# The diagonal-block forward substitution of a gated-delta network, for two batches at once on 128 lanes

## The chip, the cores and the metric

The kernel runs on one core of one Trainium2 chip. The metric is device time in microseconds (us) of one execution: median 3812.47 over three runs (3810.61 to 3817.99). PE is TensorE, DVE is VectorE, ACT is ScalarE, POOL is GpSimd, SP is SyncE, which issues the transfers (DMAs).

## The reference, cut to what matters

Two layers of a transformer-like block over 256 context tokens and 1024 latent tokens (1280 in all), width 1024, float32. A layer projects the normed tokens once; the columns go to four groups of heads (HGRN2, retention, gated delta, S5), each scanned in both directions; then an output projection and an MLP. The change lies in the gated-delta group: 4 heads of 64 columns, chunks of 64 tokens, so 20 chunk steps in a direction. Per chunk:

```
g = cumsum(log_a)
lmat = where(tri, exp(min(g_i - g_j, 0)), 0)
a_mat = where(strict, (k*beta) @ k^T * lmat, 0)
u, w = solve(a_mat + I, [v*beta, k*beta*exp(g)])      # unit lower triangular, 64x64
qk = where(tri, q @ k^T * lmat, 0);  q_dec = q*exp(g)
v_new = u - w @ s
o = q_dec @ s + qk @ v_new
s = s*exp(g_last) + k_dec^T @ v_new                   # the state, chunk after chunk
```

## The kernel before, in words

Each layer runs in stages. The stage that matters here has two streams of work. One is the gated-delta group: `gdn_conv` (a convolution on DVE, transposes `gd_pt` on PE, products of keys `gd_kk`, kept in DRAM as `kk` and `kv`), `gdn_stats` (the cumulated decays: products `gd_g` on PE, copies `gd_gp` and `gd_gc` on DVE, decay rows kept in DRAM as `gr`), and `gdn_main`, the 20 steps. The other, called the filler, is the rest of the input projections (`proj_steps`, products `pj_ps` at L1608 with evictions `pj_z`): hundreds of matrix products of 512, 272 or 256 columns that depend on nothing in the group. They are laid between the group's products, and all of them must be done before the stage's tiles are freed and the next stage begins.

`gdn_main` handles the 20 steps in five batches of four (`BS`). For a batch, `front` (L794) loads the key products M, the query products A and the queries QD, and the decay rows E; DVE subtracts (L824), ACT takes Abs and Exp, DVE and POOL multiply M (L826, L827), A (L829, L830) and QD (L822) by decays. The inverse of each unit triangular 64x64 block is built from 32x32 blocks. The two diagonal ones are inverted by forward substitution: 4 steps x 2 directions x 4 heads x 2 diagonal blocks = 64 small matrices, each laid flat on one lane (partition) of the tile `gd_TL`. To get there M is written to the DRAM scratch `lanes` (four DMAs, L838) and read back (L840). The substitution is 60 DVE instructions (L846 multiplies into `gd_tmp`, L847 adds, j = 1..30), each needing the one before it. Then a transposing copy `gd_TLt` (L850), two writes to DRAM and twelve loads into the tiles `gd_TT` and `gd_XX`. `back` (L866) computes the off-diagonal block from these on PE (32 products `gd_py` L877, 32 `gd_pz`). `step` (L898) is the chain: products `gd_p` with the state (L919), DVE `gd_pre` (L924), products with the inverse (L933), DVE `gd_Vn` (L936), products into the new state (L944), DVE `gd_S` (L950, L952), and the outputs `gd_po`.

The order on every engine is fixed when the program is built: a scheduler simulates the program and lays each engine's instructions in one sequence, in which they then run. Steps have priority over fronts, and the filler has the lowest. Tiles of one name share buffers in rotation: `gd_M` has 3, `gd_E` 2, `gd_ge` 1. In layer 0 every batch has A and QD; in layer 1 the first batch has none, since the context's output is not needed there.

Of the kernel before, what the change touches and what calls it, by code (L numbers as in the profile page):

```python
# [16 lines left out]
def host_consts():  # L17
# [4 lines left out]
    c['sel8'] = (np.arange(8)[:, None, None] == np.arange(4)[None, :, None] * 2 + (i // 64)[None, None, :]).astype(f)  # L22
# [125 lines left out]
def hgrn(k, l, need_ctx):  # L148
# [11 lines left out]
    def products(key, query, other=0):  # L160
        """key^T query per 64 tokens: partition (token half, key), free (head pair, 128 tokens, head parity, query)"""
# [289 lines left out]
def hg_params(k):  # L451
    """forget gate constants a = (1-lb)/2, b = (1+lb)/2 per layer"""
# [33 lines left out]
def ret_params(k):  # L486
    """log decays, per head on every partition [l, d, h] and per partition pair [l, d, k]"""
# [16 lines left out]
def ret_tables(k):  # L504
    """decay tables of both layers: within a chunk [head pair, head, query], of queries [d, head pair, query], of keys [d, head]"""
# [200 lines left out]
def gdn_stats(k, l):  # L706
    """decays and step sizes per step, head pair and direction"""
# [73 lines left out]
def gdn_main(k, l, need_ctx, fp):  # L781
    """chunked delta rule: both directions and all heads step together"""
# [11 lines left out]
    def front(b0):  # L794
        full = need_ctx or b0 >= 4
        w = {}
        lo = [min(chunk_of(b0, d), chunk_of(b0 + BS - 1, d)) for d in range(2)]
        quad = lambda nm, bufs, f=early: f(nm, [128, 2, BS, 2, 64], bufs)
        by_chunk = lambda a, d: a[:, b0:b0 + BS, :, d] if d == 0 else rev(a[:, b0:b0 + BS, :, d], 1)
        half = [128, BS, 2, 64]  # L800
        M = w['M'] = quad('gd_M', k.gM)
        tiles = [(M, k.kk[l][:, :, 0])]
        if full:
            A, QD = w['A'], w['QD'] = quad('gd_A', k.gA), quad('gd_QD', k.gQ)
            tiles += [(A, k.kk[l][:, :, 1]), (QD, k.kv[l][:, :, 3])]
        for t, src in tiles:
            for d in range(2):
                nc.sync.dma_start(t[:, d].rearrange('p n h c -> p n (h c)'),
                                  src[lo[d]:lo[d] + BS].rearrange('n p h c -> p n (h c)'))
        Es = []  # L810
        for d in range(2):
            Es.append(early('gd_E', half, 2))
            for y in range(2):
                nc.sync.dma_start(Es[d][64 * y:64 * y + 64].rearrange('p n h c -> p (n h c)'),
                                  bc(k.gr[l][y:y + 1, d, lo[d]:lo[d] + BS].rearrange('a n h c -> a (n h c)'), [64, BS * 128]))
        for d in range(2):
            E = Es[d]
            ef = E.rearrange('p n h c -> p (n h c)')
            if full:
# [3 lines left out]
            nc.vector.tensor_tensor(E, E, bc(by_chunk(Gp, d)[:, :, :, None], half), op=SUB)  # L823
# [3 lines left out]
            nc.gpsimd.tensor_tensor(M[:, d], M[:, d], bc(by_chunk(B2, d)[:, :, :, None], half), op=MULT)  # L827
            if full:
                nc.vector.tensor_tensor(A[:, d], A[:, d], bc(k.c['gmask'][:, d, None, None], half), op=MULT)  # L829
                nc.gpsimd.tensor_tensor(A[:, d], A[:, d], E, op=MULT)  # L830
        lanes = k.lanes[k.li % len(k.lanes)]
        k.li += 1
        blk = lambda y, b: (slice(64 * y + 32 * b, 64 * y + 32 * b + 32), slice(32 * b, 32 * b + 32), (2 * y + b) * 16)
        flat = lambda a: a.rearrange('p d n h c -> p (d n h) c')
        for y in range(2):
            for b in range(2):
                p, c, L0 = blk(y, b)
                nc.sync.dma_start(lanes[0, L0:L0 + 16].rearrange('x r c -> r x c'), flat(M[p])[:, :, c])  # L838
        TL, tmp = ln('gd_TL'), early('gd_tmp', [128, 256], 1)
        nc.sync.dma_start(TL[:nl], lanes[0])  # L840
        diag = lambda t: t[:nl].rearrange('p r c -> p (r c)')[:, ::33]
        eng = nc.gpsimd if b0 // BS in k.psolve else nc.vector
        for j in range(1, 31):
            sh = [nl, 31 - j, j]
            u = tmp[:nl, :(31 - j) * j].rearrange('p (r c) -> p r c', c=j)
            eng.tensor_tensor(u, bc(TL[:nl, j + 1:, j:j + 1], sh), bc(TL[:nl, j:j + 1, :j], sh), op=MULT)  # L846
            eng.tensor_tensor(TL[:nl, j + 1:, :j], TL[:nl, j + 1:, :j], u, op=ADD)  # L847
        nc.gpsimd.memset(diag(TL), 1.0)
        TLt = ln('gd_TLt')
        nc.vector.tensor_copy(TLt[:nl], TL[:nl].rearrange('p r c -> p c r'))  # L850
        nc.sync.dma_start(lanes[1], TLt[:nl])
        nc.sync.dma_start(lanes[2], TL[:nl])
# [11 lines left out]
        return w  # L864
# [152 lines left out]
def s5_params(k):  # L1017
# [67 lines left out]
    def dbl(c, s):  # L1085
        """angle doubling"""
# [69 lines left out]
def s5_views(t):  # L1156
    """views of the parts of a quarter's tables"""
# [5 lines left out]
def s5_tables(k, l):  # L1163
    """per quarter (4 groups) of a layer: input, output and block matrices and powers of the state's decay"""
# [106 lines left out]
def s5(k, l, need_ctx):  # L1271
# [12 lines left out]
    def blocks_of(tl):  # L1284
        """tokens in blocks of 8: U [128 (token of the block, channel), group, block]"""
# [172 lines left out]
def split_st(k, st, shape):  # L1458
    """float32 -> (hi, lo) float32r tiles whose sum is exact"""
# [17 lines left out]
def mm3(k, out, terms):  # L1477
    """accumulates hi*hi + hi*lo + lo*hi over (whi, wlo, xhi, xlo), one yield per product"""
# [18 lines left out]
def modulation(k, l, r, mp, wtag, tag='mo'):  # L1497
    """a third of the shift, scale and gate vectors, channel major: k.mod[l] [128, 2 (latent, context), 48]; one yield per weight tile"""
# [31 lines left out]
def square(k, acc, x, kt, b0, bn):  # L1530
    """adds the squares of channel tile kt of the tokens [b0, b0+bn) to acc"""
# [11 lines left out]
def rnorm(k, acc, b0, bn):  # L1543
    """PSUM tile with 1/rms of the tokens [b0, b0+bn) on every partition"""
# [15 lines left out]
def norm_mod(k, X, acc, l, part, b0, bn, H):  # L1560
    """H[kt] = split of modulated norm of a block of X; part 0: first norm, 3: second"""
# [27 lines left out]
def proj_steps(k, l, H, rows, need_ctx):  # L1589
    """projections of rows, one yield per matrix product; the first two block by block"""  # L1590
# [72 lines left out]
def within(k, gen, tp, tag):  # L1663
    """runs a generator with its own pool and PSUM tag"""
# [9 lines left out]
def weave(a, b, n, c=(), m=0):  # L1674
    """a step of a, then n of b and m of c"""
# [16 lines left out]
def load_a(k, l, kts, pool, nt, blocks, pair):  # L1692
    """splits of mixer outputs"""
# [15 lines left out]
def w_out(k, l, A, blocks, start, done, few=False):  # L1709
    """start(m, block) gives the tile that the product with the rows of A is added to, done(m, block, tile) takes it"""  # L1710
# [37 lines left out]
def mlp(k, l, H, X, blocks, final):  # L1748
    """X += gated MLP; final(m, b0, bn) after the last change of a part of X, final(None, b0, bn) after a block's"""
# [64 lines left out]
def program(k):  # L1814
    from contextlib import ExitStack
    nc, tc = k.nc, k.tc
    with ExitStack() as es:
# [16 lines left out]
        k.lanes = [k.dp.tile([3, 64, 32, 32], F32, name=f'lanes{i}') for i in range(10)]  # L1834
# [42 lines left out]
        for n in ('hmask', 'heads', 'gtri', 'gmask', 'sel8', 'dmask', 'lmask'):  # L1877
# [107 lines left out]
def tune(k):  # L1985
# [7 lines left out]
    k.psolve = ()  # L1993
# [56 lines left out]
```

## Time and profile before

| | us |
|---|---|
| median of the runs | 3812.47 |
| profiled execution, span | 3814.3 |
| PE busy | 3424.2 (90%) |
| DVE busy | 2178.1 (57%) |
| POOL busy | 1148.5 |
| ACT busy | 1108.1 |
| PE's granted clock, mean | 0.940 |

The profiled execution's span of 3814.3 us is 1.8 above the median and within the range of the runs. PE is the busiest engine over the whole span, but the share of one engine is a mean over stages; the two gated-delta stages lie at about 277 to 726 us (layer 0) and 2279 to 2683 us (layer 1), and have to be read by themselves.

### The profile page before, as it was taken

What the parts mean: (1) busy time and instruction counts of PE and PEld (TensorE: products, weight loads), DVE (VectorE), ACT (ScalarE), POOL (GpSimd) and SP (SyncE); (2) the same over time, 40 slices, a digit from 0 to 9 for tenths busy, and PEclk for the clock granted to TensorE, in tenths of its full rate; (3) what the DMA queues carried; (4) which work ended last, traced back from release to release, by engine and by line L of the source; (5) the groups of instructions that cost most, each with busy time, mean ns of one, the idle gap of its engine ahead of it and who ended that gap; (6) DMA issues with size and microseconds to landing.
All of it is one profiled execution on the core that took longest, in us unless ns stands there. A gap on an engine that the chain in (4) does not pass through costs nothing. (4 is left out here: it accounts for less than half of the span.)

```text
span 3814.3 us, 60239 instructions
## 1 busy us (share of the span) xinstructions
PE 3424.2 (90%) x23367; PEld 2725.9 (71%) x23367; DVE 2178.1 (57%) x4171; ACT 1108.1 (29%) x1988; POOL 1148.5 (30%) x1202
## 2 busy tenths in 40 slices
PE   6887899788889999999998886999787799999997
PEld 3776778555667888888886785777356578888886
DVE  8968651586665344344336979741786654334445
ACT  5332212355333211221123333111463232221222
POOL 3734322254223111111112745221552231111111
PEclk7988999989999999999999988999899899999998
DMA  6565444756641111111112556444846311111111
GB/s 211 184 164 142 134 123 137 240 152 194 197 149 37 39 37 37 39 39 39 39 37 85 162 160 171 134 114 136 253 126 224 126 41 49 50 48 47 50 45 64
DMA packets 421279, 424.76 MB, mean 111 GB/s; under 512 B 185592, under 2 KB 299128, under 8 KB 419968
## 3 DMA queue, kind: packets, MB, share of 16 engines
q1 hardware_dynamic: 420992, 420.91, 36.1%
q8 instruction: 184, 3.01, 0.3%
q14 instruction: 103, 0.84, 0.1%
HBM read 308.56 MB, written 112.22 MB: 110 GB/s over the span
## 5 line engine op out<-in xcount | busy, mean ns | idle before, releaser
L1482 PE MATMUL dn_ps<-hid,w_hi 128*128 128x512 f32 (+1 forms) x2560 | 728.4, 373 | 7.9 <-DVE x L1780 7.6
L1780 DVE SCALAR_TENSOR_TENSOR x<-dn_ps,mod,x 128x512 f32<-128x512 f32 (+1 forms) x640 | 433.1, 695 | 324.3 <-PE dn_ps L1482 323.7
L1467 POOL TENSOR_TENSOR w_lo<-w_st,w_hi 128x512 fp32r<-128x512 f32 (+1 forms) x212 | 288.6, 1364 | 992.4 <-ACT w_hi L1464 978.3
L1482 PEld LDWEIGHTS dn_ps<-hid,w_hi 128*128 128x128 f32 x2560 | 463.4, 189 | 98.4 <-DVE x L1780 9.2
L1464 ACT ACTIVATE w_hi<-w_st 128x512 fp32r<-128x512 f32 (+2 forms) x408 | 249.6, 621 | 811.8 <-PE dn_ps L1482 276.3
L1482 PE MATMUL up_ps<-hlo,w_hi 128*128 128x512 f32 (+1 forms) x1280 | 475.8, 372 | 3.4 <-DVE hlo L1578 1.9
L1482 PE MATMUL up_ps<-hhi,w_hi 128*128 128x512 f32 (+1 forms) x1280 | 476.7, 373 | 2.0 <-ACT hhi L1577 2.0
L1482 PE MATMUL up_ps<-hhi,w_lo 128*128 128x512 f32 (+1 forms) x1280 | 476.2, 372 | 0.0
L1482 PE MATMUL dn_ps<-hid,w_lo 128*128 128x512 f32 (+1 forms) x1280 | 469.0, 373 | 0.0
L1608 PE MATMUL pj_ps<-hhi,w_hi 128*128 128x512 f32 (+1 forms) x960 | 369.7, 386 | 26.4 <-ACT pj_z L1586 9.5
L1608 PE MATMUL pj_ps<-hlo,w_hi 128*128 128x512 f32 (+1 forms) x960 | 367.9, 383 | 1.8 <-DVE hlo L1578 1.8
L1608 PE MATMUL pj_ps<-hhi,w_lo 128*128 128x512 f32 (+1 forms) x960 | 366.0, 382 | 1.0 <-POOL w_lo L1467 1.0
L1467 DVE TENSOR_TENSOR w_lo<-w_st,w_hi 128x512 fp32r<-128x512 f32 (+1 forms) x196 | 148.6, 763 | 314.8 <-ACT w_hi L1464 300.5
L1765 POOL TENSOR_TENSOR up_q<-up_r 128x256 f32<-128x256 f32 (+1 forms) x160 | 156.1, 976 | 566.5 <-ACT up_r L1764 479.4
L1482 PEld LDWEIGHTS up_ps<-hlo,w_hi 128*128 128x128 f32 x1280 | 242.5, 189 | 49.2 <-DVE hlo L1578 3.5
L1482 PEld LDWEIGHTS up_ps<-hhi,w_hi 128*128 128x128 f32 x1280 | 242.5, 190 | 46.5 <-ACT hhi L1577 2.8
L1482 PEld LDWEIGHTS up_ps<-hhi,w_lo 128*128 128x128 f32 x1280 | 242.2, 189 | 44.1
L1482 PEld LDWEIGHTS dn_ps<-hid,w_lo 128*128 128x128 f32 x1280 | 240.8, 189 | 45.9
L1767 DVE TENSOR_TENSOR hid<-up_q,hid 128x256 fp32r<-128x256 f32 (+1 forms) x160 | 114.1, 721 | 278.1 <-ACT hid L1766 276.0
L1608 PEld LDWEIGHTS pj_ps<-hhi,w_hi 128*128 128x128 f32 x960 | 191.2, 199 | 63.6 <-ACT pj_z L1586 10.9
L1608 PEld LDWEIGHTS pj_ps<-hlo,w_hi 128*128 128x128 f32 x960 | 191.6, 200 | 34.5 <-DVE hlo L1578 2.4
L1608 PEld LDWEIGHTS pj_ps<-hhi,w_lo 128*128 128x128 f32 x960 | 190.6, 199 | 35.6 <-issue 3.1
(401 smaller groups left out, 5964.2 us busy)
## 6 DMA issues: line engine op xcount, KB each, us to landing
w_st<-in_w SPq DMA_DIRECT2D x256, 256.0 KB, 2.6
w_mo<-in_mod_w SPq DMA_DIRECT2D x160, 256.0 KB, 3.4
w_st<-in_w_ch SPq DMA_DIRECT2D x88, 256.0 KB, 3.3
z<-pj_z SPq DMA_DIRECT2D x88, 256.0 KB, 2.9
gd_KV<-kv SPq DMA_DIRECT2D x80, 192.0 KB, 2.9
s_ta<-s5t SPq DMA_DIRECT2D x8, 1152.0 KB, 7.3
w_mo<-in_mod_w SPq DMA_DIRECT2D x16, 512.0 KB, 7.4
at<-a SPq DMA_DIRECT2D x32, 256.0 KB, 4.5
```

The costliest lines, as they stand in the source:

```text
L1464: nc.scalar.activation(fl(hi), fl(st), AF.Copy)
L1467: eng.tensor_tensor(fl(lo), fl(st), fl(hi).bitcast(F32), op=SUB)
L1482: k.nc.tensor.matmul(out, w, x, start=(i + j == 0), stop=(i == n - 1 and j == 2))
L1608: nc.tensor.matmul(ps[:, :n], x, y, start=(kt == 0 and i == 0), stop=(kt == 7 and i == 2))
L1765: nc.gpsimd.tensor_tensor(q[:, :bn], r[:, :bn], r[:, :bn], op=MULT)
L1767: nc.vector.tensor_tensor(lo[:, sl], q[:, :bn], hi[:, sl].bitcast(F32), op=SUB)
L1780: nc.vector.scalar_tensor_tensor(X(m)[:, sl], ps[:, :bn], g, X(m)[:, sl], op0=MULT, op1=ADD)
```

## The change: what it does

`front` becomes four functions. `front_m` loads M and E and multiplies M; `front_a` does A and QD, and now loads the decay rows a second time into `gd_ge` (two buffers in place of one), where before ACT computed `gd_ge` from the E tile; `solve` does the forward substitution for one batch or two; `inverses` loads `gd_TT` and `gd_XX`. `solve` runs on batches 0 and 1 together, then 2 and 3, then 4 alone, so the 60 instructions appear three times a layer in place of five, on 128 lanes in the paired cases. The scratch `lanes` is 6 tensors of 128 lanes in place of 10 of 64. A constant that nothing used (`sel8`) and a switch that chose DVE or POOL for the substitution go. The rest of the diff empties docstrings. A new layer's order: `front_m` and `front_a` of batches 0 and 1, `solve` of both, `inverses` of both, `back(0)`; then, while batch b is stepped, `inverses(b+1)`, and for even b the fronts of b+2 and b+3 and their `solve` (`front_a` of b+3 one batch later).

```diff
-    def front(b0):
-        full = need_ctx or b0 >= 4
...
-        Es = []
+    def decays(t, lo, d):
+        for y in range(2):
+            nc.sync.dma_start(t[64 * y:64 * y + 64].rearrange('p n h c -> p (n h c)'),
+                              bc(k.gr[l][y:y + 1, d, lo:lo + BS].rearrange('a n h c -> a (n h c)'), [64, BS * 128]))
+    def front_m(b):
...
+        load(M, k.kk[l][:, :, 0], lo)
+        Es = [early('gd_E', half, 2) for d in range(2)]
+        for d in range(2):
+            decays(Es[d], lo[d], d)
         for d in range(2):
...
-            if full:
-                ge = early('gd_ge', half, 1)
-                nc.scalar.activation(ge.rearrange('p n h c -> p (n h c)'), ef, AF.Exp)
-                nc.gpsimd.tensor_tensor(QD[:, d], QD[:, d], ge, op=MULT)
...
+    def front_a(b, w):
...
+            ge = early('gd_ge', half, 2)
+            decays(ge, lo[d], d)
+            gf = ge.rearrange('p n h c -> p (n h c)')
+            nc.scalar.activation(gf, gf, AF.Exp)
+            nc.gpsimd.tensor_tensor(QD[:, d], QD[:, d], ge, op=MULT)
...
+    def solve(ws):
+        n = nl * len(ws)
...
+        for i, w in enumerate(ws):
+            w['lanes'] = lanes[:, nl * i:nl * i + nl]
...
-        nc.sync.dma_start(TL[:nl], lanes[0])
+        nc.sync.dma_start(TL[:n], lanes[0, :n])
...
         for j in range(1, 31):
-            sh = [nl, 31 - j, j]
+            sh = [n, 31 - j, j]
...
+    def inverses(w):
...
-    fr = {0: front(0), 1: front(BS)}
+    for b in range(2):
+        fr[b] = front_m(b)
+        front_a(b, fr[b])
+    solve([fr[0], fr[1]])
+    for b in range(2):
+        inverses(fr[b])
     back(fr[0])
     for b in range(n):
-        if b + 2 < n:
-            fr[b + 2] = front((b + 2) * BS)
+        if b and b + 1 < n:
+            inverses(fr[b + 1])
+        if b % 2 and b + 2 < n:
+            front_a(b + 2, fr[b + 2])
+        pair = [x for x in (b + 2, b + 3) if x < n] if b % 2 == 0 else []
+        for x in pair:
+            fr[x] = front_m(x)
+            if x == b + 2:
+                front_a(x, fr[x])
+        if pair:
+            solve([fr[x] for x in pair])
```

In SP's order of layer 0, before, the four writes of batch 0's M to `lanes` are followed by a few loads and the load of `gd_TL`:

```order
L814 DMA gd_E<-gr_79 64x512 x3
L838 DMA lanes_96<-gd_M 32x16x32 x4
L814 DMA gd_E<-gr_79 64x512
L1613 DMA zr_73<-pj_z 128x256 x3
L840 DMA gd_TL<-lanes_96 64x1024
```

After, at the same place (the first `gd_TL` load of the layer; `gd_ge` are the decay rows loaded a second time):

```order
L857 DMA lanes_96<-gd_M 32x16x32 x4
L800 DMA gd_M<-kk_88 128x4x128 x2
L800 DMA gd_A<-kk_88 128x4x128 x2
L804 DMA gd_E<-gr_79 64x512 x2
L800 DMA gd_QD<-kv_92 128x4x128 x2
L804 DMA gd_ge<-gr_79 64x512 x4
L804 DMA gd_E<-gr_79 64x512
L857 DMA lanes_96<-gd_M 32x16x32 x4
L804 DMA gd_E<-gr_79 64x512
L804 DMA gd_ge<-gr_79 64x512
L859 DMA gd_TL<-lanes_96 128x1024
```

The load of `gd_TL` now stands behind the second batch's writes, and behind the loads of a third batch. From the `gr` writes to this load SP issues 54 DMAs in place of 40 in layer 0, and 48 in place of 37 in layer 1.

On DVE at the end of the first substitution of layer 0, before, the second substitution follows at once:

```order
L846 TENSOR_TENSOR gd_tmp<-gd_TL 64x30
L847 TENSOR_TENSOR gd_TL<-gd_TL,gd_tmp 64x30
L850 COPY gd_TLt<-gd_TL 64x1024
L846 TENSOR_TENSOR gd_tmp<-gd_TL 64x30
L847 TENSOR_TENSOR gd_TL<-gd_TL,gd_tmp 64x30
L846 TENSOR_TENSOR gd_tmp<-gd_TL 64x58
```

After, at the same place (`gd_Vs`, `gd_Vn` and `gd_S` are step 0 of the chain):

```order
L864 TENSOR_TENSOR gd_tmp<-gd_TL 128x30
L865 TENSOR_TENSOR gd_TL<-gd_TL,gd_tmp 128x30
L868 COPY gd_TLt<-gd_TL 128x1024
L822 TENSOR_TENSOR gd_M<-gd_M,gd_E 128x512 x2
L1619 COPY pj_z<-pj_ps 128x512
L930 TENSOR_TENSOR gd_Vs<-gd_KV,gd_st 128x256
L956 TENSOR_TENSOR gd_Vn<-gd_p_3437,gd_st 128x256
L958 TENSOR_SCALAR gd_Vn<-gd_Vn 128x256
L972 COPY gd_S<-gd_p_3437 128x256
L864 TENSOR_TENSOR gd_tmp<-gd_TL 128x30
```

The second batch's substitution is gone from here; what follows is the M of batch 3, step 0, and then the substitution of batches 2 and 3, whose instructions stand among those of step 1. On PE, the number of filler products ahead of the layer's first `gd_py` falls: in layer 0 by 15 products of 512 columns, in layer 1 by 45 of 512 and 21 of 256 columns. In layer 0, 156 filler products of 272 and 256 columns now stand between the last key products `gd_kk` and `gd_g`, where 10 stood before.

## Rows read from the trace of the kernel before

**Rows 1.** By stretch: length; busy PE, PEld, DVE, ACT, POOL; granted clock, DMA share, GB/s.
```profile
277.00:354.40 77.40, 49.54 (x277) 43.82 (x275) 65.08 (x97) 24.80 (x43) 39.47 (x35) 0.80 0.66 168
354.40:560.00 205.60, 185.98 (x2275) 149.76 (x2275) 138.20 (x350) 42.39 (x84) 61.69 (x72) 0.93 0.48 129
560.00:640.00 80.00, 80.00 (x827) 66.46 (x824) 14.28 (x45) 14.21 (x30) 15.56 (x17) 1.00 0.30 94
2362.00:2560.00 198.00, 181.61 (x1991) 143.85 (x1989) 128.85 (x338) 38.71 (x75) 58.43 (x68) 0.94 0.46 126
2560.00:2660.00 100.00, 100.00 (x988) 72.61 (x989) 17.71 (x52) 16.81 (x33) 19.23 (x21) 1.00 0.43 128
```

**Rows 2.** The substitution's instructions grouped by line: count, busy us, mean ns, idle before.
```profile
L847 DVE TENSOR_TENSOR gd_TL<-gd_TL,gd_tmp 64x30 f32<-64x30 f32 (+5 forms) x300 | 132.4, 441 | 8.7
L846 DVE TENSOR_TENSOR gd_tmp<-gd_TL 64x30 f32<-64x30 f32 (+5 forms) x300 | 129.3, 431 | 44.4 <-DMA gd_TL<-lanes 35.8
```

**Rows 3.** PE's waits, 354.4 to 560 us (layer 0): us in total, times, longest.
```profile
PE gd_py L877 <- DMA gd_TT<-lanes: 5.2, 5, 1.7
PE gd_p L933 <- DVE gd_pre L924: 3.8, 3, 1.8
PE gd_p L944 <- DVE gd_Vn L936: 3.0, 2, 1.7
PE gd_py L877 <- DMA gd_XX<-lanes: 2.8, 3, 1.9
```

**Rows 4.** PE's waits, 2362 to 2560 us (layer 1).
```profile
PE gd_p L919 <- DVE gd_S L950: 7.5, 3, 4.3
PE gd_py L877 <- DMA gd_TT<-lanes: 4.8, 3, 3.2
PE gd_p L933 <- DVE gd_pre L924: 1.9, 1, 1.9
```

**Rows 5.** DVE's timeline, two instructions on 64 and on 128 lanes: start, duration.
```profile
320.47 0.41 DVE L910 TENSOR_TENSOR gd_Vs<-gd_KV,gd_st 128x256 f32<-128x256 f32 x1
...
327.15 0.40 DVE L846 TENSOR_TENSOR gd_tmp<-gd_TL 64x238 f32<-64x238 f32 x1
```

**Rows 6.** Busy time of the instructions on `gd_tmp`, first and third substitution of layer 0.
```profile
305.80:348.10 42.30, 33.93 (x60) 0.89 0.54 144
387.70:417.40 29.70, 22.41 (x60) 1.00 0.48 134
```

**Rows 7.** PE's timeline: `gd_g`, a wait, and the first `gd_py` of either layer.
```profile
260.35 0.89 PE L760 MATMUL gd_g<-gd_st,c_gtri 64*64 64x40 f32 x16 [4.13 <-ACT gd_tk L696]
...
304.34 0.58 PE L1608 MATMUL pj_ps<-w_hi,hhi 128*128 128x256 f32 x1 [3.89 <-ACT pj_z L1586]
...
354.56 0.24 PE L877 MATMUL gd_py<-gd_TT,gd_M 32*32 32x32 f32 x2
...
2363.39 0.24 PE L877 MATMUL gd_py<-gd_TT,gd_M 32*32 32x32 f32 x2
```

**Rows 8.** Busy time of the filler's products (L1608): 512 columns, then 256, twice.
```profile
350.00:354.40 4.40, 4.40 (x21) 1.00 0.70 152
270.20:276.00 5.80, 5.80 (x51) 1.00 0.85 237
304.90:308.10 3.20, 3.20 (x17) 0.50 0.48 128
```

**Rows 9.** SP's timeline: the second batch's writes to `lanes`; layer 1's first `gd_TL` load.
```profile
315.06 0.43 SPq L838 DMA_DIRECT2D lanes<-gd_M  x1
...
2307.77 0.48 SPq L840 DMA_DIRECT2D gd_TL<-lanes  x1
...
2314.95 1.98 SPq L838 DMA_DIRECT2D lanes<-gd_M  x4
```

**Rows 10.** DVE's timeline: first instruction of layer 1's first substitution; end of layer 0's.
```profile
2313.94 1.02 DVE L846 TENSOR_TENSOR gd_tmp<-gd_TL 64x30 f32<-64x30 f32 x1
...
346.94 1.12 DVE L850 COPY gd_TLt<-gd_TL 64x1024 f32<-64x1024 f32 x1
```

More of the change, by code (lines that the diff above doesn't have):

```diff
@@ L792, in gdn_main, with load @@
     Sst = []
-    def front(b0):
-        full = need_ctx or b0 >= 4
[L796 to L802, printed above, removed]
-        if full:
[L804 to L809, printed above, removed]
-        Es = []
-        for d in range(2):
[L812 to L815, printed above, removed]
+    quad = lambda nm, bufs, f=early: f(nm, [128, 2, BS, 2, 64], bufs)
+    by_chunk = lambda a, b0, d: a[:, b0:b0 + BS, :, d] if d == 0 else rev(a[:, b0:b0 + BS, :, d], 1)
+    half = [128, BS, 2, 64]
+    lows = lambda b0: [min(chunk_of(b0, d), chunk_of(b0 + BS - 1, d)) for d in range(2)]
+    def load(t, src, lo):
+        for d in range(2):
+            nc.sync.dma_start(t[:, d].rearrange('p n h c -> p n (h c)'), src[lo[d]:lo[d] + BS].rearrange('n p h c -> p n (h c)'))
+    def decays(t, lo, d):
[3 more added lines that the diff above has]
+    def front_m(b):
+        b0 = b * BS
+        lo = lows(b0)
+        M = quad('gd_M', k.gM)
+        load(M, k.kk[l][:, :, 0], lo)
+        Es = [early('gd_E', half, 2) for d in range(2)]
+        for d in range(2):
+            decays(Es[d], lo[d], d)
         for d in range(2):
@@ L818, in front @@
             ef = E.rearrange('p n h c -> p (n h c)')
-            if full:
-                ge = early('gd_ge', half, 1)
-                nc.scalar.activation(ge.rearrange('p n h c -> p (n h c)'), ef, AF.Exp)
-                nc.gpsimd.tensor_tensor(QD[:, d], QD[:, d], ge, op=MULT)
-            nc.vector.tensor_tensor(E, E, bc(by_chunk(Gp, d)[:, :, :, None], half), op=SUB)
+            nc.vector.tensor_tensor(E, E, bc(by_chunk(Gp, b0, d)[:, :, :, None], half), op=SUB)
             nc.scalar.activation(ef, ef, AF.Abs)
@@ L826, in front @@
             nc.vector.tensor_tensor(M[:, d], M[:, d], E, op=MULT)
[L827 to L830, printed above, removed]
+            nc.gpsimd.tensor_tensor(M[:, d], M[:, d], bc(by_chunk(B2, b0, d)[:, :, :, None], half), op=MULT)
+        return dict(M=M, Es=Es)
@@ new lines, in front_a @@
+    def front_a(b, w):
+        b0 = b * BS
+        if not (need_ctx or b0 >= 4):
+            return
+        lo = lows(b0)
+        A, QD = w['A'], w['QD'] = quad('gd_A', k.gA), quad('gd_QD', k.gQ)
+        load(A, k.kk[l][:, :, 1], lo)
+        load(QD, k.kv[l][:, :, 3], lo)
+        for d in range(2):
+            ge = early('gd_ge', half, 2)
[3 more added lines that the diff above has]
+            nc.gpsimd.tensor_tensor(QD[:, d], QD[:, d], ge, op=MULT)
+            nc.vector.tensor_tensor(A[:, d], A[:, d], bc(k.c['gmask'][:, d, None, None], half), op=MULT)
+            nc.gpsimd.tensor_tensor(A[:, d], A[:, d], w['Es'][d], op=MULT)
@@ L831, in front @@
+    blk = lambda y, b: (slice(64 * y + 32 * b, 64 * y + 32 * b + 32), slice(32 * b, 32 * b + 32), (2 * y + b) * 16)
+    def solve(ws):
+        n = nl * len(ws)
         lanes = k.lanes[k.li % len(k.lanes)]
         k.li += 1
-        blk = lambda y, b: (slice(64 * y + 32 * b, 64 * y + 32 * b + 32), slice(32 * b, 32 * b + 32), (2 * y + b) * 16)
         flat = lambda a: a.rearrange('p d n h c -> p (d n h) c')
[L835 to L838, printed above, removed]
+        for i, w in enumerate(ws):
+            w['lanes'] = lanes[:, nl * i:nl * i + nl]
+            for y in range(2):
+                for b in range(2):
+                    p, c, L0 = blk(y, b)
+                    nc.sync.dma_start(w['lanes'][0, L0:L0 + 16].rearrange('x r c -> r x c'), flat(w['M'][p])[:, :, c])
@@ L848, in front @@
         nc.gpsimd.memset(diag(TL), 1.0)
         TLt = ln('gd_TLt')
-        nc.vector.tensor_copy(TLt[:nl], TL[:nl].rearrange('p r c -> p c r'))
-        nc.sync.dma_start(lanes[1], TLt[:nl])
-        nc.sync.dma_start(lanes[2], TL[:nl])
+        nc.vector.tensor_copy(TLt[:n], TL[:n].rearrange('p r c -> p c r'))
+        nc.sync.dma_start(lanes[1, :n], TLt[:n])
+        nc.sync.dma_start(lanes[2, :n], TL[:n])
+    def inverses(w):
+        lanes = w['lanes']
         TT = w['TT'] = quad('gd_TT', k.gT, tile_)
@@ L972, in gdn_main @@
     n = 20 // BS
-    fr = {0: front(0), 1: front(BS)}
+    fr = {}
+    for b in range(2):
+        fr[b] = front_m(b)
+        front_a(b, fr[b])
+    solve([fr[0], fr[1]])
+    for b in range(2):
+        inverses(fr[b])
     back(fr[0])
     for b in range(n):
-        if b + 2 < n:
-            fr[b + 2] = front((b + 2) * BS)
+        if b and b + 1 < n:
[9 more added lines that the diff above has]
+            solve([fr[x] for x in pair])
         for i in range(BS):
@@ L1833, in program @@
         xs = dt('xs', [8, 128, T])[0]
-        k.lanes = [k.dp.tile([3, 64, 32, 32], F32, name=f'lanes{i}') for i in range(10)]
+        k.lanes = [k.dp.tile([3, 128, 32, 32], F32, name=f'lanes{i}') for i in range(6)]
         k.toep = [k.dp.tile([2, 16, 2, 240], F32, name=f'toep{i}') for i in range(8)]
@@ L1876, in program @@
                 norm_mod(k, lambda kt: xt[kt], acc, 0, 0, *b, H)
-        for n in ('hmask', 'heads', 'gtri', 'gmask', 'sel8', 'dmask', 'lmask'):
+        for n in ('hmask', 'heads', 'gtri', 'gmask', 'dmask', 'lmask'):
             load_const(k, n)
@@ L1992, in tune @@
     k.nln, k.nvs = 3, 1
-    k.psolve = ()
     k.hiprio = 6000
```

11 lines of the change are left out of this document (4 added, 7 removed).

## The prediction

> **What bounds the kernel now.** I read the busy shares of the page first: PE 90%, DVE 57%. That alone says that DVE work saved is not time saved, but it is a mean over stages, so next come the busy times by stretch around the two gated-delta stages [rows 1]. Each stage has three parts. Before the chain (277 to 354.4 us in layer 0) DVE is the busiest, 65.08 of 77.40 us, and PE waits: 49.54 busy, clock 0.80. In the chain (354.4 to 560, and 2362 to 2560) PE is busy 185.98 of 205.6 and 181.61 of 198.0 us, at clock 0.93 and 0.94. After it (560 to 640, 2560 to 2660) PE is busy 80.00 of 80 and 100.00 of 100 us at clock 1.00: that is filler, products that have to be finished before the next stage, long after the last substitution. So the end of a stage is set by PE: it comes when PE has done a fixed amount of work, and moves only by what PE idles before it, or runs at the lower clock. Then I read what PE waits for in the chain [rows 3, 4], the cost of the substitution itself [rows 2, 5, 6], and what leads to the first product of the chain [rows 7 to 10].
>
> What can be won in the chain at most is therefore PE's idle time, 205.60 - 185.98 = 19.6 us in layer 0 and 198.00 - 181.61 = 16.4 in layer 1, and the time at the lower clock, (1 - 0.93) x 205.6 = 14.4 and (1 - 0.94) x 198 = 11.9 [rows 1].
>
> **What the change removes.** Two layers x two substitutions x 60 = 240 DVE instructions. The 600 of before cost 132.4 + 129.3 = 261.7 us, or 0.436 each [rows 2], and lanes don't cost: an instruction on 256 elements took 0.41 us on 128 lanes, one on 238 elements 0.40 on 64 [rows 5]. So DVE loses 240 x 0.436 = 104.7 us of work. Of the end that is worth only what PE waited for it. PE's waits in layer 0 [rows 3]: 5.2 + 2.8 us for the blocks' landing (`gd_TT`, `gd_XX`), 3.8 for `gd_pre` and 3.0 for `gd_Vn`, short DVE operations that queue behind substitutions. With two substitutions fewer among the steps I let 11.5 of these 14.8 us go; the rest is the pair of batches 2 and 3, whose instructions still stand among those of step 1. In layer 1 [rows 4] 4.8 + 1.9 = 6.7 us are of that kind, of which I let 6 go; the 7.5 us for `gd_S` are as long as all the others, and L950 adds a tile that POOL scales, so I count none of them, and all of them as the other bound. Sum: 17.5 us, 25 at the most. I take 20.
>
> The clock: of the 14.4 + 11.9 = 26.3 us at the lower clock a third would come back if about half of the waits go and the small products of the steps stay: 9 us, between 0 and 13. The Trainium skill, page "TensorE: Matmul & The Clock Gate", Part 1 (The HAM clock gate), says that the low clock is the default and that activity lifts it; by that rule a wait is paid twice. The trace agrees: after the wait of 3.89 us at 304.34 the filler's products run at clock 0.50 [rows 7, 8]. By that rule it also speaks against this change, which makes one long wait per layer longer, as follows.
>
> **What the change adds, before the chain.** The first substitution now needs the M of batches 0 and 1, so the first `gd_py` comes later, and fewer filler products stand ahead of it on PE. Both make PE idle, and that idle is not given back, since the end is PE's work.
>
> Layer 0. Fewer products: 15 of 512 columns at 4.40 / 21 = 0.21 us [rows 8] = 3.1 us. The later start: 156 filler products stand ahead of `gd_g` in place of 10; 146 more at 5.80 / 51 = 0.114 us [rows 8] are 16.6 us, of which 4.13 fill PE's present wait there [rows 7], so `gd_g` and all that follows it is 12.5 us later. If the whole chain to the first `gd_py` (354.56) moves by that, and SP's 14 more DMAs ahead of the `gd_TL` load add 14 x 0.45 = 6.3 us [rows 9], it starts 18.8 us later. For the other end: batch 1's M is written to `lanes` at 315.06 [rows 9]; 12.5 later, and 9.3 earlier because the substitution that ran on DVE from 305.80 [rows 6] no longer stands before it, 318.3; from SP's issue to the substitution's first instruction 6.2 us (2307.77 to 2313.94 [rows 9, 10]); the substitution 29.7 us end to end, as the third [rows 6] (the first took 42.3, beside other DVE work); and 354.56 - 346.94 = 7.6 from the copy to the first `gd_py` [rows 7, 10]. That is 361.8, or 7.2 later. I take 10, nearer to the low end, since DVE idles 12.3 us in this stretch [rows 1] and can take some of the delay: 13 us of idle with the 3.1, bounds 10 and 22.
>
> Layer 1. Fewer products: 45 x 0.21 + 21 x 0.114 = 11.8 us. The later start: batch 1's writes end at 2314.95 + 1.98 = 2316.93 [rows 9], + 6.2 + 29.7 + 7.6 = 2360.4, 3 us before the present 2363.39 [rows 7]; with 42.3 for the substitution and 11 more DMAs at 0.45 it is 2378, 15 after. I take 3 after: 15 us with the 11.8, bounds 9 and 27.
>
> The clock after these waits: at 0.50, 17 products of 256 columns take 3.20 us [rows 8] where 51 take 5.80, so 3.2 - 17 x 0.114 = 1.3 us a layer; 2.6 in all, from 0 to 3.
>
> Sum of the added: 13 + 15 + 2.6 = 31 us (19 to 52).
>
> **What costs nothing.** 36 more loads of decay rows for `gd_ge`, and 13 fewer DMAs elsewhere: those in front of the first `gd_TL` load are counted above; the others lie under the chain, where the DMA share is 0.48 and 0.46 [rows 1]; if that cover were gone, 36 x 0.45 = 16 us of SP's queue would stand in front of step loads, which is part of the slower rival. ACT's work is the same in number; POOL loses four instructions.
>
> **The wait that is added inside the chain.** The pair (2,3) needs batch 3's M, whose buffer is the one of batch 0 and is freed by `back(0)`. On DVE, M of batch 3 stands after the first `gd_TLt` and ahead of step 0's `gd_Vs`, `gd_Vn` and `gd_S`; behind it waits the whole chain. Nothing in the trace shows that wait; its bounds are 0 and about the way from a freed M to a substitution, some 12 us a layer (6.2 us of transfer and start, and the loads). I take 0, because PE has filler among the steps' products; the other end is in the rival below.
>
> The sum: 31 - 20 - 9 = +2 us on the profiled execution's 3814.3, 3816; that execution is 1.8 above the median shown, so against 3812.5 it is 3814. The cause and the remedy about cancel.
>
> **The rivals.**
> - The gains alone (faster). If DVE, without a substitution between batch 0's and batch 1's fronts, has both M ready no later than now, and PE's wait ahead of the first `gd_py` grows by 3 us or less in a layer, there remain -20 - 13 + 5 = -28 us: 3785. For it: DVE idles 12.3 us in the stretch before the chain [rows 1], and the later waits in rows 3 and 4 are all shorter than 5 us each, so they can vanish. Against it: `gd_g` is 156 products down PE's queue.
> - The pair as a gate (slower). PE idles 20 us or more ahead of the first `gd_py` in each layer, and batch 3's M blocks step 0 on DVE. Price: 20 + 20 + 2.6 for the first, 12 for the second in one layer, less the 29 gained: +25 us, 3837. It decides from the point at which the first `gd_py` comes more than 12 us late in layer 0 or more than 8 in layer 1. For it: DVE's order, and SP's 54 DMAs in place of 40. Against it: the third substitution shows 29.7 us end to end [rows 6], so that a pair that runs undisturbed regains what it waited.
> - It does nothing that shows. The substitutions are hidden and the first pair is as early as now: 3812. Against it: PE's waits in rows 3 and 4 exist and their releasers change.
> - The saved DVE work is saved time. The price is the 104.7 us above: 3708. Against it: PE is busy 100% of the stretches after the chain [rows 1], so the end does not follow DVE. The Trainium skill, page "Trainium Kernel Development and Optimization", Best Practices, has as its first point to always tile to 128 partitions; read as a rule for time it gives this case. No run here shows that it pays where another engine sets the end.
>
> **How the numbers follow.** Costs and gains cancel: 0.45, with its own range from -14 to +16 us (one of the two first waits or the clock term away from the value taken), 3798 to 3829. Gains alone 0.25, gate 0.22, nothing 0.05, all of DVE's work 0.03. The predicted time is that of the first, 3814. The range is 3781 to 3841: it takes in the gate's 3837 and the first rival's 3785, and leaves about 2 in 10 beyond. A measurement of this kernel can tell some 0.2%, 7.6 us, from no change; of the first case a little over half, 0.25, lies within that, and 0.10 on either side. So faster 0.10 + 0.25 + 0.03 = 0.38, same 0.25 + 0.05 = 0.30, slower 0.10 + 0.22 = 0.32.
>
> **What would show it.** Substitution instructions 360 in place of 600, at some 0.44 us each (right if lanes are free; wrong if a paired one is longer). The first `gd_py` at about 365 us in layer 0 and 2366 in layer 1, counted from the same place in the stage, with PE idle more before it. Fewer and shorter waits of PE for `gd_TT`, `gd_XX`, `gd_pre` and `gd_Vn` in the chain, and there a clock above 0.93 and 0.94. The filler's end unmoved against the stage's start. I am wrong if the first `gd_py` is not later and PE's idle falls by 20 us or more, or if step 0 or 1 shows a wait of 10 us for DVE, or if stages outside these two change.

## The result, and the profile after

The changed kernel takes 3831.16 us (median of four runs, 3828.56 to 3835.62) against 3811.54 before (3807.56 to 3817.99): a ratio of 1.0054, 95% interval 1.0039 to 1.0068, so it is slower, by half a per cent. The time lies inside the range on record (3781 to 3841), but 17 us above the forecast of 3814, and above the 3798 to 3829 that the prediction gave to the case it forecast.

The span grew by less, from 3814.3 to 3828.9 us. The profiled execution of before was one of its longer ones: 1.8 us lie around the span after (3830.67 us for a span of 3828.9), so its own time was some 3816.1 (an estimate), 4.6 above the median of its runs. The prediction set the span against the median as if nothing lay around it.

First the substitution, in the groups of DVE after (line, operation, count, busy us, mean ns), which answer to [rows 2]:

```profile
L864 DVE TENSOR_TENSOR gd_tmp<-gd_TL 128x30 f32<-128x30 f32 (+19 forms) x180 | 76.0, 422 | 22.6 <-DMA gd_TL<-lanes 17.4
L865 DVE TENSOR_TENSOR gd_TL<-gd_TL,gd_tmp 128x30 f32<-128x30 f32 (+19 forms) x180 | 75.0, 416 | 5.4
```

360 instructions in place of 600, none dearer on 128 lanes: 151.0 us in place of 261.7, so DVE was relieved of 110.7 us. The kernel is slower all the same. The busy times by stretch after answer to [rows 1]: for each layer from `gd_g` to the first `gd_py`, the chain, and the filler behind it (length; PE, PEld, DVE, ACT, POOL busy; clock; DMA share; GB/s):

```profile
272.80:366.00 93.20, 46.65 (x312) 42.62 (x312) 65.40 (x103) 30.41 (x51) 42.18 (x35) 0.74 0.67 182
366.00:571.60 205.60, 192.18 (x2443) 156.12 (x2443) 93.19 (x241) 43.85 (x89) 61.32 (x74) 0.97 0.48 135
571.60:651.60 80.00, 80.00 (x714) 65.55 (x713) 13.10 (x39) 16.02 (x30) 14.15 (x15) 1.00 0.39 117
2274.90:2371.10 96.20, 49.33 (x312) 45.87 (x312) 62.78 (x102) 31.80 (x53) 36.12 (x34) 0.70 0.68 179
2371.10:2569.10 198.00, 191.15 (x2204) 152.65 (x2204) 90.11 (x231) 42.76 (x84) 57.08 (x69) 0.98 0.46 132
2569.10:2669.10 100.00, 100.00 (x902) 73.71 (x900) 15.12 (x46) 15.99 (x30) 19.11 (x21) 1.00 0.45 137
```

The same two stretches before the chain in the kernel before, from its `gd_g` to its first `gd_py`:

```profile
260.40:354.60 94.20, 65.28 (x410) 59.14 (x411) 70.23 (x110) 31.43 (x55) 39.47 (x35) 0.82 0.65 166
2273.90:2363.40 89.50, 61.02 (x374) 54.66 (x374) 71.22 (x111) 31.49 (x54) 42.22 (x36) 0.81 0.68 175
```

In the chain PE idles 13.4 us in place of 19.6 (layer 0) and 6.9 in place of 16.4 (layer 1), and its clock rises from 0.93 to 0.97 and from 0.94 to 0.98. Before the chain PE idles 46.6 us in place of 28.9, and 46.9 in place of 28.5. Behind the chain it is busy without a gap, as before. The last filler product of layer 0 starts at 726.8 us in place of 724.6, and that of layer 1 600.3 us after its layer's first projection product in place of 603.0: +2.2 and -2.7, so up to there the change cancels.

What is left of the 14.6 us lies in the stages behind: from the last filler product to the last product `wo_ps` of the output projection's first part. Before, layer 0, the MLP that follows, and layer 1:

```profile
724.60:1155.80 431.20, 352.48 (x2940) 246.81 (x2939) 312.52 (x621) 195.60 (x344) 159.93 (x168) 0.92 0.57 179
1155.80:2079.30 923.50, 903.27 (x4615) 765.41 (x4613) 407.05 (x626) 205.97 (x382) 172.92 (x162) 0.99 0.13 42
2682.30:3065.30 383.00, 300.02 (x2457) 204.88 (x2456) 281.25 (x549) 162.15 (x275) 160.75 (x162) 0.89 0.54 174
```

After:

```profile
726.80:1163.70 436.90, 359.69 (x2940) 252.28 (x2939) 314.87 (x622) 194.82 (x344) 159.64 (x168) 0.91 0.55 176
2686.80:3079.70 392.90, 301.67 (x2434) 209.90 (x2433) 279.55 (x546) 161.65 (x274) 148.07 (x156) 0.87 0.52 167
```

These stages (HGRN2, retention, S5, projection) are 5.7 and 9.9 us longer, though the diff doesn't touch them; the MLP is 0.7 us shorter. Their instructions are the same. In the built programs they stand in another order on every engine. In layer 0 PE idles no longer than before (77.2 us, 78.7 before), but more of its busy time lies at 1.2 GHz, the lower of the clock's two levels (a granted clock of 0.5): 57 us in place of 41. In layer 1 both grow (idle from 83.0 to 91.2 us, busy time at 1.2 GHz from 54 to 67).

### The profile page after: what moved, and what is told of

Read it like the earlier page. It is cut to its first block, busy times and chain, and to the rows that moved or that the text cites. A ratio compares the mean times of both kernels' runs of the same rounds, so it can differ in the third digit from the quotient of the medians.

```text
span 3828.9 us, 60061 instructions
## 1 busy us (share of the span) xinstructions
PE 3406.1 (89%) x23367; PEld 2718.4 (71%) x23367; DVE 2077.6 (54%) x3927; ACT 1108.6 (29%) x1988; POOL 1132.3 (30%) x1198
## 5 line engine op out<-in xcount | busy, mean ns | idle before, releaser
L1643 PEld LDWEIGHTS pj_ps<-hhi,w_hi 128*128 128x128 f32 x960 | 188.3, 196 | 72.6 <-ACT pj_z L1621 28.3
```

The costliest lines, as they stand in the source:

```text
L1643: nc.tensor.matmul(ps[:, :n], x, y, start=(kt == 0 and i == 0), stop=(kt == 7 and i == 2))
```

## What PE waits for before the chain

PE's waits after, from `gd_g` to the first `gd_py` of layer 0 (us in total, times, longest):

```profile
PE pj_ps L1643 <- ACT pj_z L1621: 24.7, 1, 24.7
PE gd_pt L656 <- ACT gd_y L641: 18.7, 1, 18.7
```

In the kernel before, from `gd_g` to the first `gd_py` of layer 0, the wait for `gd_pt` is there too, but the filler's waits are short:

```profile
PE gd_pt L657 <- ACT gd_y L642: 15.5, 1, 15.5
PE pj_ps L1608 <- ACT pj_z L1586: 6.9, 2, 3.9
PE pj_ps L1608 <- DVE pj_z L1584: 5.0, 2, 3.9
```

The long one of after is not the chain's. It is a product of the filler that waits until ACT has emptied a PSUM tile into `pj_z`. That eviction, in ACT's timeline after:

```profile
341.39 0.72 ACT L1621 ACTIVATE pj_z<-pj_ps 128x256 f32<-128x256 f32 x2 [6.59 <-DMA zr<-pj_z]
```

ACT has idled 6.59 us until a transfer `zr<-pj_z` was done: the three `pj_z` buffers are full until their stores have gone out. SP's timeline after, around PE's wait (317.1 to 341.8):

```profile
311.73 3.85 SPq L804 DMA_DIRECT2D gd_ge<-gr  x4
...
322.72 0.45 SPq L804 DMA_DIRECT2D gd_ge<-gr  x1
323.36 0.45 SPq L859 DMA_DIRECT2D gd_TL<-lanes  x1
324.39 1.09 SPq L804 DMA_DIRECT2D gd_E<-gr  x2
325.52 1.87 SPq L804 DMA_DIRECT2D gd_ge<-gr  x3
...
329.93 2.22 SPq L857 DMA_DIRECT2D lanes<-gd_M  x4
332.19 5.67 SPq L661 DMA_DIRECT2D kv<-gd_x  x7
337.91 2.59 SPq L1648 DMA_DIRECT2D zr<-pj_z  x3
```

The stores go out at 337.91, behind the decay loads, the third batch's `lanes` and seven stores of `kv`. Some of those loads had to wait for a free buffer, as SP's waits from 300 to 345 us show (L804 loads the decay rows; us, times, longest; the decay loads of the kernel before waited too, 5.3 us in all from 288 to 340 us):

```profile
SPq L804 <- POOL gd_QD L840: 4.1, 2, 2.5
SPq L804 <- DVE gd_M L822: 3.5, 1, 3.5
```

In the kernel before the stores stand among the loads of the fronts:

```profile
295.85 1.59 SPq L1613 DMA_DIRECT2D zr<-pj_z  x3
...
304.31 0.32 SPq L1613 DMA_DIRECT2D zr<-pj_z  x1
...
316.08 0.58 SPq L1613 DMA_DIRECT2D zr<-pj_z  x1
```

Layer 1 shows the same wait of PE, 28.3 us, but ACT comes to the eviction in another way, without a wait for a store: straight from a decay that was loaded a second time (`gd_ge`), whose load it had waited for. ACT's timeline after, in layer 1:

```profile
2343.28 0.63 ACT L839 ACTIVATE gd_ge<-gd_ge 128x512 f32<-128x512 f32 x1 [1.06 <-DMA gd_ge<-gr]
2343.81 0.64 ACT L1621 ACTIVATE pj_z<-pj_ps 128x256 f32<-128x256 f32 x2
```

In layer 0, too, the store explains only the last 6.59 of the 24.7 us: until 334.8 ACT is at the activations of the fronts, which stand ahead of the eviction in its order. So there are two ways from the second loads to PE's wait, by the stores on SP and by the fronts' activations on ACT. That is a reading of one profile; the experiments test the second load, and not which of the two ways it takes.

## The experiments

Two theories at first. A: the change cancels in the delta stages, and what is lost is the other order of the stages behind. B: the first pair of batches is a gate and costs the time.

**The unused constant, and the second load of the decays.** Two edits of the kernel before. The first drops the constant alone:

```diff
-        for n in ('hmask', 'heads', 'gtri', 'gmask', 'sel8', 'dmask', 'lmask'):
+        for n in ('hmask', 'heads', 'gtri', 'gmask', 'dmask', 'lmask'):
```

> The kernel before with one edit: the constant that nothing uses is not loaded. Theory A (the delta stages of the change cancel, and the loss comes from the scheduler laying the stages after them in another order): in the order of this kernel 156 filler products already stand between the last key product and gd_g in layer 0, as in the changed kernel, and the stages that follow the delta stages are laid in another order too; so gd_g starts at about 272 us in place of 260, the time from the end of the filler to the first up_ps moves by 3 to 12 us in one layer or both, in either direction, and the whole by between -8 and +15 us. Theory B (the first pair of batches is the gate and costs the time): nothing here touches the pair, so the time is that of before within 4 us, and every stage within 3 us.

3821.53 us, ratio 1.0022 (1.0012 to 1.0031). `gd_g` starts at 271.8 us: the 156 filler products that stand ahead of `gd_g` in the changed kernel come from this edit alone. That a load that nothing uses moves the time by more than 4 us speaks against B. A's sizes were too small: the stage behind the filler of layer 1 lasts 414.3 us in place of 383.0, after a filler that ends 17 us earlier in its layer.

The second edit takes, besides, the second load:

```diff
-                ge = early('gd_ge', half, 1)
-                nc.scalar.activation(ge..., ef, AF.Exp)
+                ge = early('gd_ge', half, 2)
+                for y in range(2):
+                    nc.sync.dma_start(ge[64 * y:64 * y + 64]..., k.gr[l][y:y + 1, d, lo[d]:lo[d] + BS]...)
+                gf = ge...
+                nc.scalar.activation(gf, gf, AF.Exp)
```

> The kernel before, without the unused constant, and with the decay rows loaded a second time into two gd_ge buffers (36 more loads), no batches paired. Theory A: the first gd_py comes at 350 to 362 us in layer 0; PE waits for gd_TT, gd_XX and gd_pre in the chain as before (12 us or more in layer 0); the stages after the delta stages again move by up to 12 us each. Whole: -8 to +15. Theory B: as before within 4 us.

3833.96, ratio 1.0063 (1.0049 to 1.0077): with no batch paired it is as slow as the changed kernel. Neither theory had this: A's bound was +15 and B's 4. The first `gd_py` came at 359.4, as A had it; but PE's waits for `gd_TT` in the chain of layer 0 were 1.2 us, not 12 or more with `gd_pre`.

**Pairing taken back.** Five substitutions a layer, or four (only the first two batches apart, the first part of this edit); the scratch `lanes` gets 10 or 8 tensors in place of 6:

```diff
-    solve([fr[0], fr[1]])
+    for b in range(2):
+        solve([fr[b]])
...
-        if pair:
-            solve([fr[x] for x in pair])
+        for x in pair:
+            solve([fr[x]])
```

> The changed kernel with five substitutions a layer on 64 lanes, one batch at a time, at the same places in the program. Theory A: the first gd_py is 5 to 15 us earlier than in the changed kernel in layer 0 (351 to 361), PE idles again some 6 us more a layer in the chain behind substitutions, so each delta stage ends within 5 us of the changed kernel's; the whole is 3815 to 3840, set by the stages after. Theory B: the loss goes, 3811 within 5 us, with the delta stages 8 us or more shorter than in the changed kernel.

3827.98, ratio 1.0036 (1.0023 to 1.0049), within A's numbers and far from B's; but A had the delta stages within 5 us of the changed kernel's, and they end 14.8 us later in layer 0 (741.6) and 16.5 in layer 1 (616.8 from the layer's first product). Pairing is worth more there than thought, and the stages behind hide it.

> The changed kernel with the first two batches substituted one at a time and the pair of batches 2 and 3 kept: 240 instructions a layer in place of 180. Theory A: first gd_py as in the unpaired kernel, waits in the chain as in the changed one; each delta stage 3 to 10 us shorter than in the changed kernel; the stages after move by up to 12 us each, the whole 3805 to 3835. Theory B: the pair's wait is gone and the gain stays, 3795 to 3808.

3845.74, ratio 1.0087 (1.0073 to 1.0101), slower than either theory allowed. The first `gd_py` came at 361.6, 4.4 us earlier than in the changed kernel, not the 10 that a gate would give back; and the delta stages, which A had 3 to 10 us shorter, end 9.8 us later in layer 0 (736.6) and 3.9 in layer 1.

**The stages behind, held.** Four runs settle what their order is worth. A table of the instructions' numbers, taken from another kernel's built program, is made into order edges on each engine; data and work stay as they are:

```diff
+def pin(k):
+    ins = k.nc.cur_bb.bb.instructions
+    for at, table in zip(k.marks, PINNED):
+        for order in table.values():
+            seq = [ins[at + int(x)] for x in order.split()]
+            for a, b in zip(seq, seq[1:]):
+                k.tc.add_manual_dep(b, a.name, mybir.DependencyInfo(mybir.DependencyClass.NoSync, mybir.DependencyReason.DATA), reason='pin')
```

> The changed kernel, with one thing fixed by a table: the two stages that follow the delta stages (HGRN2, retention, S5 and most of the output projection) have, on every engine, the order that they have in the kernel before. The delta stages keep the changed kernel's order. Theory A (the change cancels in the delta stages, and the loss is the other order of the stages after them): those stages lost 5.8 and 10.3 us of PE's time more than in the kernel before, so 3831 - 16 = 3815, 3808 to 3820. Theory B (the first pair as a gate; the order of later stages does not matter): 3831 within 5 us.

3818.89, ratio 1.0024 (1.0012 to 1.0036): as A had it. 12 of the 20 us are the order of two stages that the change doesn't touch.

> The mirror of it: the kernel before, with the changed kernel's order in the two stages after the delta stages. Theory A: 3812 + 16 = 3828, 3820 to 3834. Theory B: 3812 within 4 us.

3823.58, ratio 1.0038 (1.0024 to 1.0052): again 12 us, from the other side.

> The changed kernel, with the two stages after the delta stages in the order that they have in the unpaired kernel, where PE lost 13 and 20 us less in them than in the changed kernel. Theory A: 3831 - 33 = 3798, 3790 to 3810. Theory B: 3831 within 5 us.

3818.26, ratio 1.0017 (1.0008 to 1.0026): 13 us gained, not 33. That an order mattered held; that the loss read from one kernel's profile moves with its order to another kernel did not.

> The unpaired kernel with the two stages after the delta stages in the order of the kernel before: with the pinned changed kernel this shows what pairing alone is worth. Theory A: in the unpaired kernel PE lost 31 us more in the delta stages than in the changed kernel, so it comes out 25 to 35 us above the pinned changed kernel, at about 3845. Theory B: no pair has to be waited for, so it is 8 us or more below the pinned changed kernel.

3855.44, ratio 1.0117 (1.0104 to 1.0130), 36.5 us above the paired kernel in the same later order; A had 25 to 35, and B had it below. So pairing alone gains 36.5 us by the medians. The two profiles lie 27 us apart, since that of the paired kernel fell on its slowest run, 10.9 above its median; 25.8 of the 27 are there when the filler ends (9.2 in layer 0, 16.6 in layer 1). The chains of both layers, unpaired and then paired, in this order:

```profile
360.50:566.10 205.60, 187.66 (x2287) 152.98 (x2287) 135.19 (x344) 41.89 (x85) 59.71 (x72) 0.91 0.48 130
2377.20:2575.20 198.00, 184.06 (x1935) 146.84 (x1935) 124.65 (x325) 39.22 (x77) 58.07 (x69) 0.91 0.46 128
```

```profile
368.60:574.20 205.60, 195.38 (x2450) 159.45 (x2451) 92.61 (x241) 43.83 (x89) 61.31 (x74) 0.95 0.48 135
2373.20:2571.20 198.00, 189.73 (x2193) 151.25 (x2192) 90.27 (x230) 42.54 (x84) 57.26 (x69) 0.97 0.45 131
```

DVE has 42.6 and 34.4 us less to do, and PE idles 7.7 and 5.7 us less at a clock higher by 0.04 and 0.06.

B had fallen. What costs the time before the chain was still open: waiting for two batches (C, the prediction's own reason) or the second load (D). The next four hold the later order too, but for the last.

> The kernel before without the unused constant, with the two later stages held in the order of the kernel before: what dropping the constant is worth in the delta stages alone. Theory D (the time that PE loses before the chain comes from the decay rows' second load and the order laid for it, not from waiting for two batches): gd_g at about 272 us in layer 0, but 89 more filler products ahead of the first gd_py, PE loses no more than before there: 3800 to 3815. Theory C (the late gd_g of layer 0 costs what the prediction gave it, some 10 us): 3820 to 3827.

3807.39, ratio 0.9989 (0.9980 to 0.9998), within D's numbers and below C's. The late `gd_g` costs nothing: PE has more filler ahead of the first `gd_py`, as D had it.

> The kernel before without the unused constant and with the decay rows loaded a second time, nothing paired and nothing split, the later stages held in the order of the kernel before. Theory D: 138 fewer filler products ahead of the first gd_py in layer 0 than without the second load (997 against 1135) and 99 fewer in layer 1 (906 against 1005), so PE idles 15 to 20 us more in each layer before the chain: 3830 to 3845. Theory C: transfers off the path, 3812 to 3822.

3845.19, ratio 1.0086 (1.0073 to 1.0100): the second load, with its second buffer and the order that the scheduler then lays before and in the chain, costs 38 us with nothing paired. That is just above D's 3830 to 3845, and far above C's 3812 to 3822. The stretches from `gd_g` to the first `gd_py`, without the second load and then with it:

```profile
271.80:369.70 97.90, 69.69 (x417) 61.63 (x417) 74.91 (x119) 31.47 (x56) 45.62 (x39) 0.86 0.64 167
2268.80:2360.70 91.90, 62.31 (x379) 56.44 (x379) 69.75 (x112) 31.71 (x54) 42.36 (x36) 0.80 0.66 171
```

```profile
273.90:363.20 89.30, 39.72 (x278) 36.63 (x279) 68.46 (x111) 29.42 (x50) 40.68 (x35) 0.73 0.70 177
2283.00:2367.60 84.60, 39.87 (x273) 37.30 (x273) 64.71 (x116) 29.03 (x49) 33.61 (x32) 0.70 0.71 180
```

PE's idle goes from 28.2 to 49.6 us and from 29.6 to 44.7. The wait is the one found in the changed kernel, in PE's waits of layer 0:

```profile
PE pj_ps L1612 <- ACT pj_z L1590: 28.4, 1, 28.4
```

Here ACT comes to the eviction straight from a second load, as in layer 1 of the changed kernel, and it does so in both layers (ACT's timeline, layer 0):

```profile
343.03 0.63 ACT L825 ACTIVATE gd_ge<-gd_ge 128x512 f32<-128x512 f32 x1 [2.88 <-DMA gd_ge<-gr]
343.56 0.64 ACT L1590 ACTIVATE pj_z<-pj_ps 128x256 f32<-128x256 f32 x2
```

So of the four long waits in the two kernels only one, in layer 0 of the changed kernel, ends with the landing of a store. No run moves the stores alone, or the second loads to another place.

**A version from the findings.** Paired, but the queries' decays computed from the E tile as before (the second load only for the fourth batch), one `gd_ge` buffer, the constant still loaded:

```diff
+    def front_m(b, whole=False):
...
+            if whole:
+                ge = early('gd_ge', half, 1)
+                nc.scalar.activation(ge..., ef, AF.Exp)
+                nc.gpsimd.tensor_tensor(QD[:, d], QD[:, d], ge, op=MULT)
```

> A version put together from the findings: the paired substitution of the changed kernel, but the decays of the queries computed by ACT from the E tile as before (the second load only for the fourth batch, whose front is split), gd_ge with one buffer and the unused constant still loaded, so that the order before the delta stage is that of before; the later stages held in the order of the kernel before. Theory D: the chain keeps the paired gain of 25 to 30 us and the wait before the first gd_py grows by 8 us at most in both layers together: 3785 to 3800, faster than both. Theory C: waiting for two batches costs as much as the pair gains: 3807 to 3818.

3799.25, ratio 0.9963 (0.9951 to 0.9976): faster than both kernels. Its stretches before the chain, and the chains:

```profile
257.20:359.10 101.90, 74.38 (x456) 67.76 (x456) 67.69 (x104) 33.88 (x59) 42.41 (x37) 0.82 0.62 168
2262.80:2363.10 100.30, 67.06 (x390) 60.13 (x391) 64.96 (x103) 32.94 (x56) 41.39 (x37) 0.78 0.64 169
359.10:564.70 205.60, 192.38 (x2447) 156.92 (x2448) 90.98 (x241) 43.95 (x89) 61.78 (x73) 0.96 0.48 135
2363.10:2561.10 198.00, 190.21 (x2167) 150.17 (x2166) 87.22 (x228) 42.83 (x82) 58.58 (x70) 0.97 0.46 131
```

Both batches are still waited for, yet PE idles 27.5 and 33.2 us before the chain, against 28.9 and 28.5 in the kernel before: the wait for two batches costs some 3 us of idle in both layers of this version together. The chains keep the paired gain.

> The same version with the later stages as the scheduler lays them. Theory D: the held one's time plus or minus 15 us. Theory C: 3812 plus or minus 15 us.

3822.71, ratio 1.0026 (1.0015 to 1.0037): 23 us above the held one, more than the 15 that D allowed; the time alone would fit C's 3812 plus or minus 15, which the held run has ruled out. The scheduler's own order for the later stages gives back all that the version gains.

At one later order, the steps from before to after are: the constant dropped -5.5 us against its runs of before (3807.39 and 3812.92), the second load +38 (3845.19), the split front and its order of calls +10 (3855.44; not taken apart further), pairing -36.5 (3818.89), and then the scheduler's own later order +12 (3831.16). That is 18 in sum, where 19.6 were measured; the steps compare medians of different series.

## Why the prediction was right or wrong

- **What bounds the kernel**: right up to the end of the filler. PE is busy 100% behind the chain in both layers; 110.7 us of DVE work went and the kernel became slower. The rival that took it for time is out. But that the next stage follows the filler's end is too strong: without the constant, and with the later order held, the last filler product of layer 0 starts 21.9 us earlier than in the kernel before (702.7), and the last `wo_ps` comes at 1157.6 in place of 1155.8.
- **The gain in the chain**: 20 us of waits were forecast and 6.2 + 9.5 = 15.7 came; the clock was to give 9 and gave (0.97 - 0.93) x 205.6 + (0.98 - 0.94) x 198 = 16.1 by the prediction's measure, which counts PE's idle time at the lower clock as well. PE's busy time at 1.2 GHz fell from 46.6 to 19.9 us in the two chains; half of that difference, 13.3 us, is the time gained, an estimate from the two levels of 1.2 and 2.4 GHz. The sum, 29.0 against 29, is right by two errors of opposite sign.
- **The cost before the chain**: the size was near, the cause wrong. 31 us were forecast; PE's idle from `gd_g` to the first `gd_py` grew by 17.6 + 18.4 = 36.0 us. The first `gd_py` came at 366.0 (365 forecast) and, less the 7.2 us by which layer 1 began later, at 2363.9 (2366). But the prediction laid it to the wait for batch 1's M and to the late `gd_g`. The late `gd_g` cost nothing (3807.39), and waiting for both batches about 3 us; the filler stood at one eviction, behind the second loads. The wait of 4.1 us ahead of `gd_g` fell to 0.8, as the prediction had it. Its clock term, 2.6 us of cost, had the wrong sign: PE's busy time at 1.2 GHz before the chain fell from 31.6 to 25.0 us, a gain of 3.3. With these, 36.0 - 3.3 - 3.3 - 29.0 leaves 0.4 us; the filler's ends, +2.2 and -2.7, give -0.5.
- **"What costs nothing"** is the step that failed here: the 36 loads of decay rows. They were weighed by their share of the DMA engines and by SP's issue time, 16 us at the most, and not by what stands behind them in the engines' orders: the stores of `pj_z` on SP, and on ACT the evictions for which PE's filler waits. Loaded a second time, the rows cost 38 us in the held order (3807.39 to 3845.19). How much of that goes by SP and how much by ACT is not shown.
- **The term that was missing**: stages outside the two were taken to stay. They are 5.7 + 9.9 = 15.6 us longer, which is more than the whole growth of the span, 14.6, since the delta stages end 0.5 us earlier in sum. This is where the forecast of "no change" broke; the text named it as a sign of being wrong, and gave it no price.
- **The gate** (slower, 3837) comes nearer in time than the forecast and is wrong in mechanism: taken apart, the pair costs 36.5 us more. Its own sign did not come either: the first `gd_py` was 11.5 and 0.5 us late, where it asked for more than 12 and 8. The range had been drawn to take in this rival's number, and only so does it hold the measured time, which is luck.
- **The clock and the long wait**: the stretches before the chain run at 0.74 and 0.70 in place of 0.82 and 0.81, but that mean counts the idle time itself; PE's busy time at 1.2 GHz did not grow there in sum, as said above. The prediction named the Trainium skill, "TensorE: Matmul & The Clock Gate", Part 1 (The HAM clock gate), for the low clock being the default that activity lifts. For a single wait the trace agrees: behind the one of 24.7 us the products of 256 columns start 0.21 us apart, against 0.114 us each at the full clock [rows 8]. That a longer wait costs more at the lower clock is not borne out: one long wait stands here in place of several short ones.

Open: which instruction of the later stages loses the 12 us. Their order was held as a whole, never in part. Holding it also shifts the first part of layer 1 a little, and in kernels whose filler ends early some of the gain is lost again behind it, as below. It is also not shown why the scheduler lays the stores and the evictions behind the second loads.

In the held version from the findings the last filler product of layer 0 starts at 695.1 us, 29.5 earlier than before, but the last `wo_ps` at 1145.8, only 9.9 earlier. From its last filler product to its first HGRN2 product (at 730.4; in the kernel before 738.8, 14.2 us after the filler) it has:

```profile
695.00:730.40 35.40, 17.63 (x139) 7.71 (x138) 17.10 (x32) 7.28 (x12) 8.88 (x9) 0.77 0.84 254
```

PE is busy half of this stretch and no engine more than half; the DMA share is 0.84. What PE waits for there:

```profile
PE hg_pa L172 <- POOL hg_ks L198: 10.5, 1, 10.5
PE mod_ps L1555 <- DMA w_mo<-in_mod_w: 6.0, 3, 3.7
```

The first wait is there in the kernel before too, with 10.2 us; the second, for weights of the modulation, is not. So in this version the first HGRN2 product comes when these are there, 8.4 us earlier than in the kernel before, and not when PE has done its filler.

## What to carry to other kernels

Price a transfer by what stands behind it, in the order of the engine that issues it and of the engine that uses it, and not by its bytes: here, with 36 more loads, the busiest engine stood 25 to 28 us at one eviction in each layer, and the kernel took 38 us longer. Where a scheduler lays the whole program, an edit also reorders stages that it doesn't touch; hold their order, in both kernels, before a gain or loss of half a per cent is put down to the edit. Here the scheduler's own later order was from 27 us faster (the unpaired kernel) to 23 us slower (the version from the findings) than the held one.

## What was not expected of the hardware

The paired instructions are no dearer: 422 and 416 ns on 128 lanes against 431 and 441 on 64. That they look cheaper is not an effect of the lanes: in the held pair of kernels they took 424 and 412 ns on 128 lanes, and 411 and 421 on 64. And the time hangs on order as much as on work: the kernel without the unused constant took 3821.53 us in one order of its later stages and 3807.39 in another, with the same instructions.
